# A hybrid decoder layer on one core: retention outputs turned into DRAM by VectorE, their gate moved to GpSimd in the last stage

## The chip, the cores and the metric

The kernel runs on one core of a Trainium2 chip. The time is device time of one execution in microseconds (us). Three runs of the kernel before took 2121.14, 2123.21 and 2124.8 us. The engines are PE (TensorE; PEld is its weight load), DVE (VectorE), ACT (ScalarE), POOL (GpSimd) and SP (SyncE, which here only issues DMAs). ACT and SP issue DMAs, each from its own instruction stream.

## The reference, cut to what matters

The layer has two branches on one normalised input: retention with 4 heads and latent attention (MLA). For the change only the retention branch counts. Per head, 1024 prompt tokens go through in chunks of 128, with a state of 256 x 512 that is carried on:

```
scores  = (q @ k.T) * dmask                       # 128 x 128
o       = scores @ v + (q @ s_prev) * q_decay     # 128 tokens x 512
s_new   = g**128 * s_prev + (k * k_decay).T @ v   # 256 x 512
on      = (o - mean(o)) * rsqrt(var(o) + EPS)     # per token and head
ret_out = on * gn_w * silu(rg)                    # rg: the gate path of the input projection
h_ret   = ret_out @ w_down_ret                    # 2048 -> 1024
merged  = sigmoid(ga) * h_ret + sigmoid(gb) * h_mla
```

Each head also has 32 sample tokens (8 sequences of 4) with states of their own. Data are fp32; products are made of two parts, a rounded `hi` and a rest `lo`, in three matmuls.

## The kernel before, in words

`mac` (L263) makes the three matmuls: L267 hi x hi, L268, L269. A 128-token chunk's product with 512 columns is one such triple per 128 rows of depth. The stages follow each other in the span: input norm and projections; the gate paths beside the sample's attention (to about 665 us), which leave sigmoid inputs `ga`, `gb`, the gates `mg` and the silu of the retention gate `gt` in DRAM; retention, head by head (665 to 1323); MLA of the prompt (1323 to 1625); and the last stage, in which `w_down_mla` (8 steps f), `w_down_ret` (2 halves of 8 steps) and `w_out` follow (from 1625 on).

Retention: `head_qk` (L823) projects q and k in three column tiles; each is rotated by DVE and POOL (L845 to L850), the rotated k is turned in blocks of 32 (L856) and stored to `kD` by SP (L858), and at the end of the three tiles the sample's columns are copied by ACT (`kS`, L866). `values_of` (L876) makes the values of one chunk in 8 triples, ACT casts them (`vnh`, L884), DVE takes the rest (`vnl`, L200). `front` makes scores (L939) and the decayed keys (`knh`, `knl`). `back` makes scores x values, q x old state, and keys x values into new states; then `group_norm` (L888 to L902: statistics on DVE, one power on POOL, and on ACT the row `on`, 128 tokens x 512). The steps of `back` of one chunk are woven by numbers with those of `values_of` of the next. `gate_in` (L905) loads a chunk's 128 x 4 x 128 of `gt`; `gate_out` turns `on` by four transposes on PE (L915; for the sample four products with a selecting matrix, L917), multiplies by weight and gate on DVE (L919) and stores to `go` by SP (L921). Under a head's last chunks lies the sample's state (`sample_state`, L1037); while it runs, PE is filled up with the next head's projections, in the last head with `mg`.

In the last stage, step f of `w_down_mla` loads `gate` (L1494, ACT takes its sigmoid), runs 3 column thirds of 24 matmuls, and DVE takes each third times the gate out of PSUM (L1515). Beside it a 128 x 1056 piece of `go` is loaded into `gl` (L1478), cast by ACT (`gh`, L1197) and reduced to the rest by DVE (L200).

A scheduler orders each engine's instructions beforehand, from its own estimates; on the chip every engine runs its list in order. A DMA also waits until the transfer before it on its completion lane has landed; eight lanes (DMAHW0 to DMAHW7) are shared by SP's and ACT's DMAs. PSUM has 2 buffers `mm`, 3 `ac`, 3 `tr`.

Of the kernel before, what the change touches and what calls it, by code (L numbers as in the profile page):

```python
# [162 lines left out]
def decode_step(ctx: ExitStack, tc: tile.TileContext, A: dict, O: dict):  # L163
# [17 lines left out]
    def tr():  # L181
        return banks["pool"].tile([P, 512], F32, tag="tr", name="tr", bufs=3)
# [16 lines left out]
    def lo_of(out, src, hi):  # L199
        dve.tensor_tensor(out=out, in0=src, in1=b32(hi), op=ALU.subtract)  # L200
# [16 lines left out]
    gaD = [dram.tile([P, NT], F32, tag=f"ga{f}", name=f"ga{f}") for f in range(8)]  # L217
    gbD = [dram.tile([P, NT], F32, tag=f"gb{f}", name=f"gb{f}") for f in range(8)]
    mgD = [dram.tile([P, NT], F32, tag=f"mg{f}", name=f"mg{f}") for f in range(8)]
    gtD, goD = ([dram.tile([P, 4, NT], F32, tag=f"{n}{h}", name=f"{n}{h}") for h in range(HR)] for n in ("gt", "go"))  # L220
    latD = dram.tile([NLAT // 32, 32, SEQ], F32, tag="latD", name="latD")
    xTD = dram.tile([P, 8, NT], F32, tag="xTD", name="xTD")
    pTD = dram.tile([PLE // 32, 32, NT], F32, tag="pTD", name="pTD")
# [224 lines left out]
    def chain(*gs):  # L448
        for g_ in gs:
            yield from g_  # L450
# [425 lines left out]
    def values_of(c, X, V):  # L876

        ps = mm()
        for k in range(8):
            mac(ps, tuple(x[:, c * P:(c + 1) * P] for x in xn[k]), X["W"][k], k == 0, k == 7)  # L880
            if k < 7:
                yield 0.69
        vh, vl = V[c] = pair("vn", DV, 2)
        act.copy(vh, ps)  # L884
        lo_of(vl, ps, vh)
        yield 0.69

    def group_norm(po, n, qd, qd2):  # L888
# [13 lines left out]
        act.activation(on[:n], po, AF.Identity, bias=nb[:n], scale=s[:n])  # L902
        return on

    def gate_in(h, n, cols):  # L905
        g = p4.tile([P, 4, P], F32, tag="g", name="g", bufs=3)[:, :, :n]
        sp.dma_start(g, gtD[h][:, :, cols])
        return g

    def gate_out(h, on, n, cols, g):  # L910
        pt = tr()
        for f in range(4):
            o = pt[:, f * P:f * P + n]
            if n == P:
                pe.transpose(o, on[:, f * P:(f + 1) * P], ident)  # L915
            else:
                pe.matmul(o, on[:, f * P:(f + 1) * P], C("sel"), start=True, stop=True)  # L917
        for f in range(4):
            dve.scalar_tensor_tensor(out=g[:, f, :], in0=pt[:, f * P:f * P + n], scalar=gnw[:, 4 * h + f:4 * h + f + 1],  # L919
                                     in1=g[:, f, :], op0=ALU.mult, op1=ALU.mult)  # L920
        sp.dma_start(goD[h][:, :, cols], g)  # L921

    def pair(name, w, bufs, rows_=P):
        return tuple(p4.tile([rows_, w], F32R, tag=name + s, name=name + s, bufs=bufs) for s in "hl")

    def prompt_chunks(h, X):
        q, k = X["q"], X["k"]
        V = {}
        gC = float(np.exp(P * lg[h]))
        S = p4.tile([P, 2 * DV], F32, tag="S", name="S", bufs=1)  # L930
        T = {}
        kd = C("kd", h, 1)

        def front(c):

            sl = slice(c * P, (c + 1) * P)
            pss = ac()
            for m in range(2):
                pe.matmul(pss[:, :P], k[m][:, sl], q[m][:, sl], start=m == 0, stop=m == 1)  # L939
            smh, sml = pair("sm", P, 2)  # L940
            sm = p4.tile([P, P], F32, tag="smr", name="smr", bufs=1)
            dve.tensor_tensor(out=sm, in0=pss[:, :P], in1=C("maskT", h, P), op=ALU.mult)
            act.copy(smh, sm)
            lo_of(sml, sm, smh)
            kh, kl = pair("kn", DK, 2)
            if c:
                kn = b32(kl)
                sp.dma_start(kn, kD[h % 2][4 * c:4 * c + 4].rearrange("b i f -> (b i) f"))
            else:
                kn = tr()[:, :DK]  # L950
                for m in range(2):
                    pe.transpose(kn[:, m * P:(m + 1) * P], k[m][:, sl], ident)
            act.activation(kh, kn, AF.Copy, scale=kd)
            dve.scalar_tensor_tensor(out=kl, in0=kn, scalar=kd, in1=b32(kh), op0=ALU.mult, op1=ALU.subtract)
            return smh, sml, kh, kl

        def back(c, parts):
            sl = slice(c * P, (c + 1) * P)
            smh, sml, kh, kl = parts
            vh, vl = V.pop(c)  # L960
            if c:
                qh, ql = pair("qc", DK, 1)
                for m in range(2):
                    ms = slice(m * P, (m + 1) * P)
                    hi_pool(qh[:, ms], q[m][:, sl])
                    lo_of(ql[:, ms], q[m][:, sl], qh[:, ms])
            g = gate_in(h, P, sl)
            po = ac()
            mac(po, (smh, sml), (vh, vl), True, c == 0)
            yield 0.65  # L970
            for m in range(2 if c else 0):
                Sh, Sl = T["S"]
                ms, vs = slice(m * P, (m + 1) * P), slice(m * DV, (m + 1) * DV)
                mac(po, (qh[:, ms], ql[:, ms]), (Sh[:, vs], Sl[:, vs]), False, m == 1)
                yield 0.65
            for m in range(2):
                ms, vs = slice(m * P, (m + 1) * P), slice(m * DV, (m + 1) * DV)
                pS = ac()
                mac(pS, (kh[:, ms], kl[:, ms]), (vh, vl), True, True)
                if c:  # L980
                    dve.scalar_tensor_tensor(out=S[:, vs], in0=S[:, vs], scalar=gC, in1=pS, op0=ALU.mult, op1=ALU.add)
                else:
                    act.copy(S[:, vs], pS)
                yield 0.65
            if c < 7:
                Sh, Sl = T["S"] = tuple(p4.tile([P, 2 * DV], F32R, tag="st", name=f"St{n}", bufs=4) for n in "hl")
                for m in range(2):
                    vs = slice(m * DV, (m + 1) * DV)
                    hi_pool(Sh[:, vs], S[:, vs])
                    lo_of(Sl[:, vs], S[:, vs], Sh[:, vs])  # L990
            on = group_norm(po, P, C("qd", h, 1), C("qd2", h, 1))
            yield None
            gate_out(h, on, P, sl, g)
            yield 0.43

        def ahead(u):

            for cost in u:
                if cost is None:
                    return  # L1000
                yield cost

        parts = front(0)
        yield 1.0
        yield from values_of(0, X, V)
        while late:
            gate_out(*late.pop())
        due = iter(())
        for c in range(8):
            if c == 7:  # L1010
                X["st"] = [states(h, 0, 0)]
            u = back(c, parts)
            if c < 7:
                parts = front(c + 1)
                yield 1.0
                yield from woven((chain(due, ahead(u)), 3.9), (values_of(c + 1, X, V), 5.5))
                due = u
        yield None
        yield from due
        yield from ahead(u)  # L1020
        X["st"].append(states(h, 0, 1))
        yield from u
        sp.dma_start(O["ret_prompt"][0, 0, h].rearrange("(m p) e -> p m e", p=P), S.rearrange("p (m e) -> p m e", m=2))
# [13 lines left out]
    def sample_state(h, X):  # L1037

        q, k = X["qS"], X["kS"]
        g4 = float(np.exp(NS * lg[h]))  # L1040
        sl = slice(SEQ, NT)

        def weights(k):
            raw = p4.tile([P, DV], F32, tag="vn" + "hl"[k % 2], name="wvS", bufs=2)
# [27 lines left out]
        yield 2.5  # L1072
        ps = ac()
        for n in range(8):
            for r in range(4):
# [9 lines left out]
        yield 1.0  # L1085
# [15 lines left out]
        g = gate_in(h, NR, sl)  # L1101
# [385 lines left out]

    def load_gated(f, pl):
        lo = gated(f, pl)
        return split_gated(pl("gh"), lo)  # L1490

    def gate(src, f):
        t = w4("gate", dt=F32)
# [27 lines left out]
    gx[7] = split_gated(xr_("gh"), gx[7])  # L1521
    merged, nxt = [], []
    for half in range(2):
        for f in range(8):
# [295 lines left out]
```

## Time and profile before

| | |
|---|---|
| median of three runs | 2123.21 us |
| the profiled execution: its own time, its span | 2122.66 us, 2120.9 us |
| PE busy | 2085.8 us (98%) |
| DVE, ACT, POOL busy | 1239.0, 699.6, 306.0 us |
| granted TensorE clock, mean | 0.997 |
| DMA, mean over the span | 152 GB/s |

Busy shares are averages over stages. Where PE has no gap, time goes only if PE's own work goes; where PE waits, the wait that ends last counts. "[0.44 <-X]" behind an instruction says that its engine sat idle for so long before it and that X released it.

### The profile page before, as it was taken

Reading aid. Unit: us, or ns where it says so; the run is one execution under the profiler, and the core shown is the slowest. Engines: PE = TensorE matmul, PEld = TensorE weight load, DVE = VectorE, ACT = ScalarE, POOL = GpSimd, SP = SyncE. Lnnn points to the kernel's source line nnn. Section 1 sums busy time; section 2 is a strip of 40 time slices with the busy share of each in tenths; the row PEclk is TensorE's granted clock in tenths of the full one; section 3 lists DMA queues with packets and bytes.
Section 4 is the critical chain, followed back from the end, with each engine's and each line's share of the span. In section 5 each row is a group of like instructions: output and inputs, shape, how many; then the busy total and the mean of one; then the engine's idle time right before and its main releaser. Section 6 shows DMA issues by size and latency. Waiting matters only on the chain. (4 is left out here: it accounts for less than half of the span.)

```text
span 2120.9 us, 38551 instructions
## 1 busy us (share of the span) xinstructions
PE 2085.8 (98%) x15282; PEld 1806.3 (85%) x15282; DVE 1239.0 (58%) x2791; ACT 699.6 (33%) x1455; POOL 306.0 (14%) x517
## 2 busy tenths in 40 slices
PE   8999999999999999999999999999999999999998
PEld 7988777777777898888888887888888999999976
DVE  6524555565655457677676774877777353454443
ACT  6312232333433232222222222454566341232221
POOL 2210111111100022222222220122211000000000
PEclk9999999999999999999999999999999999999999
DMA  7576656566565332654635647210112453336642
GB/s 206 135 242 212 238 193 233 208 246 227 193 240 182 113 87 71 206 163 140 208 87 163 195 147 251 56 48 19 39 52 81 152 181 94 95 117 133 175 151 91
DMA packets 346870, 321.91 MB, mean 152 GB/s; under 512 B 126945, under 2 KB 294049, under 8 KB 342593
## 3 DMA queue, kind: packets, MB, share of 16 engines
q1 hardware_dynamic: 320192, 213.92, 34.5%
q0 software_dynamic: 9216, 83.89, 10.6%
q10 hardware_dynamic: 17280, 21.63, 2.8%
q8 instruction: 120, 1.97, 0.4%
q14 instruction: 62, 0.50, 0.1%
HBM read 246.69 MB, written 72.69 MB: 151 GB/s over the span
## 5 line engine op out<-in xcount | busy, mean ns | idle before, releaser
L267 PE MATMUL mm<-xh,wh 128*128 128x352 f32 x1344 | 456.7, 340 | 3.9 <-ACT gev L440 2.3
L269 PE MATMUL mm<-xh,wl 128*128 128x352 f32 x1344 | 436.5, 325 | 2.1 <-DVE wl L200 2.1
L268 PE MATMUL mm<-xl,wh 128*128 128x352 f32 x1344 | 436.6, 325 | 0.0
L267 PEld LDWEIGHTS mm<-xh,wh 128*128 128x128 f32 x1344 | 253.2, 188 | 87.4 <-issue 77.2
L269 PEld LDWEIGHTS mm<-xh,wl 128*128 128x128 f32 x1344 | 254.2, 189 | 3.9 <-DVE wl L200 2.4
L268 PEld LDWEIGHTS mm<-xl,wh 128*128 128x128 f32 x1344 | 254.3, 189 | 3.4 <-issue 2.1
L688 DVE STREAM_TRANSPOSE kt<-craw 128x512 f32<-128x512 f32 x256 | 161.3, 681 | 85.9 <-PE sc L692 81.1
L200 DVE TENSOR_TENSOR wl<-wr,wh 128x512 fp32r<-128x512 f32 (+2 forms) x203 | 139.3, 699 | 98.1 <-ACT wh L248 67.1
L248 ACT CAST wh<-wr 128x512 fp32r<-128x512 f32 x150 | 90.0, 618 | 240.5 <-PE mm L268 184.6
L440 ACT ACTIVATE gev<-mm 128x352 f32<-128x352 f32 x120 | 55.5, 463 | 238.8 <-PE mm L269 218.4
L267 PE MATMUL mm<-mh,wh 128*128 128x352 f32 x384 | 124.5, 324 | 1.4 <-ACT mh L1197 0.8
L268 PE MATMUL mm<-ml,wh 128*128 128x352 f32 x384 | 124.8, 325 | 0.8 <-DVE ml L200 0.6
L269 PE MATMUL mm<-mh,wl 128*128 128x352 f32 x384 | 124.3, 324 | 0.0
L269 PE MATMUL mm<-gh,wl 128*128 128x352 f32 x384 | 124.3, 324 | 0.0
L267 PE MATMUL mm<-gh,wh 128*128 128x352 f32 x384 | 124.3, 324 | 0.0
L268 PE MATMUL mm<-gl,wh 128*128 128x352 f32 x384 | 124.2, 323 | 0.0
L267 PE MATMUL mm<-wv,xh 128*128 128x512 f32 x256 | 103.5, 404 | 0.0
L268 PE MATMUL mm<-wv,xh 128*128 128x512 f32 x256 | 100.9, 394 | 0.0
L269 PE MATMUL mm<-wv,xl 128*128 128x512 f32 x256 | 100.8, 394 | 0.0
L692 PE MATMUL sc<-kt,q 32*32 32x512 f32 x2560 | 91.2, 600 | 0.0
L902 ACT ACTIVATE on<-ac,gb,gs 128x512 f32<-128x512 f32 x36 | 28.0, 778 | 153.1 <-DVE gb L900 147.9
L267 PEld LDWEIGHTS mm<-mh,wh 128*128 128x128 f32 x384 | 72.4, 188 | 1.9 <-ACT mh L1197 1.0
(419 smaller groups left out, 4365.6 us busy)
## 6 DMA issues: line engine op xcount, KB each, us to landing
wr<-in_w_in_dram SPq DMA_DIRECT2D x144, 256.0 KB, 3.7
st<-in_state_ret_dram SPq DMA_DIRECT2D x32, 512.0 KB, 5.1
out_ret_sample_dram<-st SPq DMA_DIRECT2D x32, 512.0 KB, 3.5
gt<-gev ACTq DMA_DIRECT2D x48, 176.0 KB, 3.1
gl<-go SPq DMA_DIRECT2D x16, 528.0 KB, 5.4
gate<-ga SPq DMA_DIRECT2D x16, 528.0 KB, 3.6
g<-gt SPq DMA_DIRECT2D x32, 256.0 KB, 3.2
go<-g SPq DMA_DIRECT2D x32, 256.0 KB, 2.6
```

The source lines that it names most:

```text
L200: dve.tensor_tensor(out=out, in0=src, in1=b32(hi), op=ALU.subtract)
L248: hi_by[0](hi, raw)
L267: pe.matmul(out, wh, xh, start=first, stop=False)
L268: pe.matmul(out, wh, xl, start=False, stop=False)
L269: pe.matmul(out, wl, xh, start=False, stop=last)
L440: act.activation(t, ps, func)
L688: dve.transpose(kt[:, 2 * i + s].rearrange("p (n r) -> p n r", r=32), src)
L692: pe.matmul(sc[32 * v:32 * v + 32, q, :], Q["q4"][qs_, j + v // 2, 2 * (g % 2) + v % 2, :], kt[qs_, v, :], start=n == 0, stop=n == NJ // 2 ...
L902: act.activation(on[:n], po, AF.Identity, bias=nb[:n], scale=s[:n])
```

## The change

The four transposes and the selecting products on PE, the gate loads, the four DVE products and the SP store of each chunk go. Instead DVE turns `on` by one 128 x 512 transpose in blocks of 32 x 32 into a buffer `g`, and ACT issues four DMAs per chunk, one for each 32 partitions, which put the blocks into `go` in DRAM (16 blocks of 32 x 1056). These four are held, in program order, right behind ACT's cast of the next values. In the last stage `gated` loads the piece of `go` and also the piece of `gt` (into `rg`, one of three buffers that the gates use too), POOL multiplies them in three thirds, ACT makes `hi` with the norm's weight as its scale, and DVE the rest. In `back` keys x values come first, then the other two products; the numbers of the weave follow, and the first chunk's order is its own.

```diff
-    gtD, goD = ([dram.tile([P, 4, NT], F32, tag=f"{n}{h}", name=f"{n}{h}") for h in range(HR)] for n in ("gt", "go"))
+    gtD = [dram.tile([P, 4, NT], F32, tag=f"gt{h}", name=f"gt{h}") for h in range(HR)]
+    goD = [dram.tile([DV // 32, 32, NT], F32, tag=f"go{h}", name=f"go{h}") for h in range(HR)]
...
         vh, vl = V[c] = pair("vn", DV, 2)
-        act.copy(vh, ps)
+        tc.keep_in_program_order(act.copy(vh, ps))
         lo_of(vl, ps, vh)
+        store_out()
...
-    def gate_in(h, n, cols):
...
-    def gate_out(h, on, n, cols, g):
...
+    turned_out = []
+
+    def turn_out(h, on, n, t0):
+        st = p4.tile([P, DV], F32, tag="g", name="g", bufs=3).rearrange("p (b r) -> p b r", r=32)
+        dve.transpose(st, on.rearrange("p (b r) -> p b r", r=32))
+        turned_out.append((h, st, n, t0))
+
+    def store_out():
+        while turned_out:
+            h, st, n, t0 = turned_out.pop(0)
+            for a in range(4):
+                tc.keep_in_program_order(act.dma_start(goD[h][:, :, t0 + a * n:t0 + a * n + n].rearrange("b i t -> i b t"),
+                                                       st[32 * a:32 * a + 32, :, :n]))
...
+            old = T.get("S")
             for m in range(2):
                 ms, vs = slice(m * P, (m + 1) * P), slice(m * DV, (m + 1) * DV)
                 pS = ac()
...
+            po = ac()
+            mac(po, (smh, sml), (vh, vl), True, c == 0)
+            yield 0.65
+            for m in range(2 if c else 0):
+                Sh, Sl = old
+                ms, vs = slice(m * P, (m + 1) * P), slice(m * DV, (m + 1) * DV)
+                mac(po, (qh[:, ms], ql[:, ms]), (Sh[:, vs], Sl[:, vs]), False, m == 1)
+                yield 0.65
             on = group_norm(po, P, C("qd", h, 1), C("qd2", h, 1))
             yield None
-            gate_out(h, on, P, sl, g)
-            yield 0.43
+            turn_out(h, on, 32, c * P)
...
-                yield from woven((chain(due, ahead(u)), 3.9), (values_of(c + 1, X, V), 5.5))
+                if c:
+                    parts = front(c + 1)
+                    yield 1.0
+                coming = values_of(c + 1, X, V)
+                if c == 0:
+                    yield from islice(coming, 3)
+                both = woven((chain(due, ahead(u)), 3.5), (coming, 9.0))
...
         if h + 1 < HR:
-            late.append((h, on, NR, sl, g))
+            late.append((h, on, NS * 2, SEQ))
         else:
-            gate_out(h, on, NR, sl, g)
-            yield 0.5
+            store_out()
+            turn_out(h, on, NS * 2, SEQ)
+            store_out()
...
     def gated(f, pl):
         lo = pl("gl")
-        sp.dma_start(b32(lo), goD[f // 4][:, f % 4, :])
-        return lo
+        sp.dma_start(b32(lo), goD[f // 4][4 * (f % 4):4 * (f % 4) + 4].rearrange("b i t -> (b i) t"))
+        g = w4("rg", dt=F32)
+        sp.dma_start(g, gtD[f // 4][:, f % 4, :])
+        for j in range(3):
+            sl = slice(j * TH, (j + 1) * TH)
+            pool.tensor_tensor(out=g[:, sl], in0=b32(lo)[:, sl], in1=g[:, sl], op=ALU.mult)
+        return lo, g, gnw[:, f:f + 1]
 
-    def split_gated(hi, lo):
+    def split_gated(hi, lo, g, nw):
 
         for j in range(3):
             sl = slice(j * TH, (j + 1) * TH)
-            split(b32(lo)[:, sl], hi[:, sl], lo[:, sl])
+            act.activation(hi[:, sl], g[:, sl], AF.Copy, scale=nw)
+            dve.scalar_tensor_tensor(out=lo[:, sl], in0=g[:, sl], scalar=nw, in1=b32(hi)[:, sl], op0=ALU.mult, op1=ALU.subtract)
         return hi, lo
```

Behind L217 the changed kernel's lines are a few numbers off those of before. Three places show how instructions move.

ACT at the start of the second head, before: the casts of the first two chunks' values (`vnh`), the first state (`S`, twice) and the two copies `kS` of the sample's keys.

```order
L953 ACTIVATE knh<-tr,cst 128x256
L943 CAST smh<-smr 128x128
L884 CAST vnh<-mm 128x512
L953 ACTIVATE knh<-knl,cst 128x256
L943 CAST smh<-smr 128x128
L983 COPY S<-ac 128x512
L902 ACTIVATE on<-ac,gb,gs 128x512
L983 COPY S<-ac 128x512
L866 COPY kS<-k_9640 128x32
L884 CAST vnh<-mm 128x512
L943 CAST smh<-smr 128x128
L866 COPY kS<-k_9639 128x32
```

The same place of the changed kernel; the eight stores are those of the last two chunks of the head before.

```order
L885 CAST vnh<-mm 128x512
L918 DMA go_102<-g 32x16x32 x4
L867 COPY kS<-k_9558 128x32
L918 DMA go_102<-g 32x16x32 x3
L867 COPY kS<-k_9557 128x32
L918 DMA go_102<-g 32x16x32
L967 COPY S<-ac 128x512 x2
L941 CAST smh<-smr 128x128
L951 ACTIVATE knh<-knl,cst 128x256
L885 CAST vnh<-mm 128x512
L918 DMA go_102<-g 32x16x8 x4
L904 ACTIVATE on<-ac,gb,gs 128x512
```

The second cast of values stood ahead of the second `kS` copy; it now stands behind it, the last store, both state copies and the next chunk's `smh` and `knh`.

DVE at the same place of the changed kernel: the statistics of the first chunk's outputs (L892 to L902), the last factor of the rotation of k (`rt`, L849), which POOL turns into the key that the second `kS` copy reads, and the turns of that key.

```order
L940 TENSOR_TENSOR smr<-ac,cst 128x128
L892 BN_STATS st_10022<-ac 128x6
L894 BN_AGGR mv<-st_10022 128x2
L896 TENSOR_SCALAR gv<-mv,cst 128x1
L900 TENSOR_TENSOR gs<-gr,cst 128x1
L902 SCALAR_TENSOR_TENSOR gb<-mv,gs 128x1
L849 TENSOR_TENSOR rt_9863<-rx,sinR 128x352
L857 STREAM_TRANSPOSE kb<-k_9557 128x320
```

The factor stands behind the whole of the first chunk's statistics, which wait for the first chunk's scores x values.

ACT at the end of retention, before (the last head's sample row is `on`; `lh` is the cast of MLA's latents, with which MLA begins):

```order
L902 ACTIVATE on<-ac,gb,gs 128x512
L440 ACTIVATE gev<-mm 128x352
L441 DMA mg_97<-gev 128x352
L1197 CAST krA<-krT 128x512
L440 ACTIVATE gev<-mm 128x352
L1211 CAST lh_14270<-lat 128x256
```

and in the changed kernel, with the completion lanes that each DMA waits for:

```order
L918 DMA go_105<-g 32x16x8 [waits DMAHW3_49,DVE_49]
L918 DMA go_105<-g 32x16x8 [waits DMAHW4_49]
L918 DMA go_105<-g 32x16x8 [waits DMAHW5_49]
L918 DMA go_105<-g 32x16x8 [waits DMAHW6_49]
L441 ACTIVATE gev<-mm 128x352 [waits PE_49]
```

Twelve stores (eight of two chunks, four of the sample) now stand between `on` and the cast `lh`; lane 4, for which the second of the sample's waits, was last used by SP's load of the next `w_ukv` weights, which SP issues once DVE has split the weights before them.

SP in the last stage, before (`wr` are the next weights):

```order
L1494 DMA gate<-gb_86 128x1056
L247 DMA wr<-in_w_down_mla_dram 128x4x128 x2
L1478 DMA gl<-go_102 128x1056
L1494 DMA gate<-gb_87 128x1056
L247 DMA wr<-in_w_down_mla_dram 128x4x128 x2
L1478 DMA gl<-go_102 128x1056
```

and in the changed kernel:

```order
L1487 DMA rg<-gt_98 128x1056
L1507 DMA gate<-gb_86 128x1056
L248 DMA wr<-in_w_down_mla_dram 128x4x128 x2
L1485 DMA gl<-go_102 128x1056
L1487 DMA rg<-gt_99 128x1056
L1507 DMA gate<-gb_87 128x1056
```

Each step loads one piece more, ahead of the gate. On DVE the split of a step's `gl` stays where it was: ahead of that step's third product with the gate (L1515, then L1528).

## Rows read from the trace of the kernel before

**Rows 1.** Stretches: length; PE, PEld, DVE, ACT, POOL busy (instructions); clock, DMA, GB/s.

```profile
800.00:950.00 150.00, 149.46 (x847) 126.01 (x846) 105.03 (x246) 38.28 (x78) 36.94 (x66) 1.00 0.51 151
1630.00:1760.00 130.00, 130.00 (x806) 130.00 (x805) 60.65 (x117) 46.68 (x85) 2.61 (x1) 1.00 0.47 154
```

**Rows 2.** Line L915: durations ns min/median/max; waits before it, us, times.

```profile
L915 PE MATMUL tr<-cst,on x128: 271/273/328, 796.0 to 1277.3; 128*128 128x128 f32 x128
...
  ACT on L902: 1.5, 2
```

**Rows 3.** Timeline of PE's weight loads: start us, us, engine line op out<-in.

```profile
795.90 0.47 PEld L915 LDWEIGHTS tr<-cst,on 128*128 128x128 f32 x4
...
796.34 0.19 PEld L267 LDWEIGHTS mm<-wv,xh 128*128 128x128 f32 x1
...
924.68 1.09 PEld L917 LDWEIGHTS tr<-cst,on 128*128 128x128 f32 x8
```

**Rows 4.** Timeline at the end of a chunk's values, first head.

```profile
795.11 0.39 PE L268 MATMUL mm<-wv,xh 128*128 128x512 f32 x1
...
795.34 0.39 PE L269 MATMUL mm<-wv,xl 128*128 128x512 f32 x1
...
796.25 0.58 ACT L884 CAST vnh<-mm 128x512 fp32r<-128x512 f32 x1
...
796.86 0.69 DVE L200 TENSOR_TENSOR vnl<-mm,vnh 128x512 fp32r<-128x512 f32 x1 [0.35 <-ACT vnh L884]
```

**Rows 5.** Timeline of the last rotation of k, first head.

```profile
798.70 0.52 DVE L848 TENSOR_TENSOR rt<-rx,sinR 128x352 f32<-128x352 f32 x1
```

```profile
799.29 0.94 POOL L850 TENSOR_TENSOR k<-k,rt 128x352 f32<-128x352 f32 x1 [3.21 <-DVE rt L848]
```

**Rows 6.** Timeline of DVE in the last head's statistics.

```profile
1313.72 0.70 DVE L890 BATCH_NORM_STATS2 st<-ac 128x6 f32<-128x512 f32 x1 [2.63 <-PE ac L1109]
...
1316.72 0.17 DVE L892 BATCH_NORM_AGGREGATE mv<-st 128x2 f32<-128x6 f32 x1
...
1318.01 0.16 DVE L900 SCALAR_TENSOR_TENSOR gb<-mv,gs 128x1 f32<-128x1 f32 x1
```

**Rows 7.** Stores: the landing of L858's (128-byte runs), ACT's issue of `gt` (L441).

```profile
DMA to landing us min/median/max: 1.6/1.7/3.5
```

```profile
L441 ACTq DMA_DIRECT2D gt<-gev x48: 326/326/327, 372.2 to 646.5; - x48
```

**Rows 8.** Timeline at the end of retention; the last row: DMA, count, KB, us to landing.

```profile
1314.02 0.43 PE L267 MATMUL mm<-xh,wh 128*128 128x352 f32 x1
...
1323.32 0.32 PE L269 MATMUL mm<-xh,wl 128*128 128x352 f32 x1
...
1324.64 0.36 PE L267 MATMUL ac<-wqr,lh 128*128 128x256 f32 x1 [1.00 <-ACT lh L1211]
```

```profile
1324.52 0.38 SPq L247 DMA_DIRECT2D wr<-in_w_ukv_dram  x1
```

```profile
wr<-in_w_ukv_dram SPq DMA_DIRECT2D x2, 128.0 KB, 2.9
```

**Rows 9.** The last stage: timeline of SP, ACT and DVE; L1478's landing; POOL's L850.

```profile
1656.82 0.51 SPq L1478 DMA_DIRECT2D gl<-go  x1
...
1667.60 0.49 SPq L1478 DMA_DIRECT2D gl<-go  x1
```

```profile
1663.53 1.26 ACT L1197 CAST gh<-gl 128x352 fp32r<-128x352 f32 x3 [2.84 <-DMA gl<-go]
```

```profile
1665.36 0.52 DVE L1515 TENSOR_TENSOR M<-mm,gate 128x352 f32<-128x352 f32 x1
```

```profile
1632.34 3.04 DVE L200 TENSOR_TENSOR wl<-wr,wh 128x512 fp32r<-128x512 f32 x2 [0.44 <-ACT wh L248]
```

```profile
DMA to landing us min/median/max: 3.5/5.4/8.0
```

```profile
L850 POOL TENSOR_TENSOR k<-k,rt x12: 932/944/951, 775.9 to 1211.2; 128x352 f32<-128x352 f32 x12
```

More of the change, by code (lines that the diff above doesn't have):

```diff
@@ L903, in group_norm @@
         return on
-    def gate_in(h, n, cols):
-        g = p4.tile([P, 4, P], F32, tag="g", name="g", bufs=3)[:, :, :n]
-        sp.dma_start(g, gtD[h][:, :, cols])
-        return g
-    def gate_out(h, on, n, cols, g):
[L911 to L921, printed above, removed]
+    turned_out = []
[9 more added lines that the diff above has]
+                                                       st[32 * a:32 * a + 32, :, :n]))
     def pair(name, w, bufs, rows_=P):
@@ L960, in back @@
             vh, vl = V.pop(c)
[L961 to L975, printed above, removed]
+            old = T.get("S")
             for m in range(2):
@@ L984, in back @@
                 yield 0.65
+            if c:
+                qh, ql = pair("qc", DK, 1)
+                for m in range(2):
+                    ms = slice(m * P, (m + 1) * P)
+                    hi_pool(qh[:, ms], q[m][:, sl])
+                    lo_of(ql[:, ms], q[m][:, sl], qh[:, ms])
             if c < 7:
@@ L1006, in prompt_chunks @@
         while late:
-            gate_out(*late.pop())
-        due = iter(())
+            turn_out(*late.pop())
+        due, done = iter(()), 0.0
         for c in range(8):
@@ L1013, in prompt_chunks @@
             if c < 7:
-                parts = front(c + 1)
-                yield 1.0
-                yield from woven((chain(due, ahead(u)), 3.9), (values_of(c + 1, X, V), 5.5))
+                if c:
+                    parts = front(c + 1)
[4 more added lines that the diff above has]
+                both = woven((chain(due, ahead(u)), 3.5), (coming, 9.0))
+                for cost in both:
+                    yield cost
+                    if c == 0:
+                        done += cost
+                        if done > 3.5:
+                            parts, done = front(1), -99.0
+                            yield 1.0
                 due = u
@@ L1040, in sample_state @@
         g4 = float(np.exp(NS * lg[h]))
-        sl = slice(SEQ, NT)
         def weights(k):
@@ L1071, in sample_state @@
                 pool.tensor_copy(qm[:, m, :, i, NS * i:NS * i + NS], q[:, m].rearrange("p (r i t) -> p r i t", i=2, t=NS)[:, :, i])
-        yield 2.5
+        yield 3.5
         ps = ac()
@@ L1084, in sample_state @@
             act.copy(vs[rs, r * P:(r + 1) * P], ps[rs, :P])
-        yield 1.0
+        yield 2.0
         pt = tr()
@@ L1100, in sample_state @@
         pe.matmul(px, sm.rearrange("p r x -> p (r x)"), vs, start=True, stop=False, skip_group_check=True)
-        g = gate_in(h, NR, sl)
         out = O["ret_sample"][0].rearrange("(r i) h (m p) e -> i m h p r e", i=2, m=2)
@@ L1477, in gated @@
         lo = pl("gl")
-        sp.dma_start(b32(lo), goD[f // 4][:, f % 4, :])
-        return lo
-    def split_gated(hi, lo):
+        sp.dma_start(b32(lo), goD[f // 4][4 * (f % 4):4 * (f % 4) + 4].rearrange("b i t -> (b i) t"))
+        g = w4("rg", dt=F32)
+        sp.dma_start(g, gtD[f // 4][:, f % 4, :])
         for j in range(3):
             sl = slice(j * TH, (j + 1) * TH)
-            split(b32(lo)[:, sl], hi[:, sl], lo[:, sl])
+            pool.tensor_tensor(out=g[:, sl], in0=b32(lo)[:, sl], in1=g[:, sl], op=ALU.mult)
[5 more added lines that the diff above has]
+            dve.scalar_tensor_tensor(out=lo[:, sl], in0=g[:, sl], scalar=nw, in1=b32(hi)[:, sl], op0=ALU.mult, op1=ALU.subtract)
         return hi, lo
     def load_gated(f, pl):
-        lo = gated(f, pl)
-        return split_gated(pl("gh"), lo)
+        parts = gated(f, pl)
+        return split_gated(pl("gh"), *parts)
     def gate(src, f):
@@ L1520, in decode_step @@
     xr_ = slots(rph.enter_context(tc.tile_pool(name="x2", bufs=1, side="right")), "x2", 17)
-    gx[7] = split_gated(xr_("gh"), gx[7])
+    gx[7] = split_gated(xr_("gh"), *gx[7])
     merged, nxt = [], []
```

## The prediction, made before the changed kernel ran

> **What bounds the kernel now.** I read the busy time by stretches first. In a stretch of retention PE is busy for 149.46 of 150 us and in the last stage for 130.00 of 130, at full clock, while ACT, POOL and DVE have room [rows 1]. So in both stages time goes only if PE's own work goes or PE comes to wait. Next I read the lines that the change removes, with their waits and their place among PE's weight loads [rows 2, 3], and then, at each place where the new order puts something in a row that PE waits for, the durations of that chain [rows 4 to 9]. The sum is made against the profiled execution, 2122.66 us with a span of 2120.9; the 1.76 around the span I leave as it is. It lies 0.55 under the median of the three runs, so a time worked out from it stands for the median too.
>
> **The change part by part.**
>
> *PE's turning goes.* Four transposes hold up the next weight load from 795.90 to 796.34, 0.44 us [rows 3]; the 273 ns of one instruction overlap and are not the price [rows 2]. 128 of them are 32 x 0.44 = 14.1 us. The selecting products of a head take 1.09 [rows 3], three heads 3.3; the fourth head's stand at the end of retention, below. With them go the waits for `on`, 1.5 us [rows 2]. PE's next work is ready there, so it is all gain: -18.9, and I allow 2 us to either side.
>
> *DVE, POOL, SP in retention.* One turn on DVE in place of four products, loads and stores gone from SP: DVE was busy for 105 of 150 us [rows 1] and doesn't set the end. Nothing.
>
> *Keys x values first.* In the middle of a head the casts now have this long: after the last values matmul PE has the six matmuls of q x old state at 0.23 (795.11 to 795.34) and the scores, 0.33 (from 795.57 to the load at 795.90), 1.7 us, and one matmul more until `vnl` is read, 2.0 [rows 3, 4]. In the shown chunk the cast starts 0.68 and `vnl` ends 1.98 after the last values slot, with ACT held up a little [rows 4]. It just fits. I take nothing, and keep 0.3 per chunk as the bound: 28 chunks, 8 us. The four stores stand behind the cast, 0.33 each [rows 7], 1.3 of some 9.5 us in which ACT is a quarter busy: hidden.
>
> *The start of heads 2 to 4.* Here something is newly in a row. Count from the end of the first chunk's values. PE does 57 matmuls, 13.25, and two pairs of scores, 0.66, until it wants the second chunk's `vnh` at 13.9, and `vnl` one matmul later. DVE: scores x values of the first chunk end at 8.0 (33 matmuls, one pair of scores); its statistics take 0.70 and 1.45 [rows 6], to 10.15, and only then comes the last factor `rt`, 0.59 until POOL starts, 0.94 there [rows 5]: 11.7. Behind that key ACT has the copy, one store, two state copies, `smh` and `knh`, 2.3 us (0.33 for the store, 0.4 for each of the others, an estimate under the 0.58 of the larger cast [rows 4, 7]), then the cast: 14.0 to 14.6, and `vnl` by 15.3. PE waits 0.7 and then 0.5, 1.2 us a head, three heads: +3.6. If ACT is quicker or the factor earlier it is 0; with 0.58 for every one and stores of 0.5, as SP's longest here [rows 9], 2.6 a head: 8.
>
> *The end of retention.* Before, 10.62 us lie between the last state product's successor and MLA's first matmul (1314.02 to 1324.64) [rows 8], filled by 48 matmuls of `mg`. The new order leaves 39 there, so 9 x 0.161 (130 us for 806 matmuls [rows 1]) = 1.45 us of work have gone ahead. The new chain from the same point: 39 matmuls 6.3; SP issues the `w_ukv` load 1.04 behind the last of them (1323.48 to 1324.52); it lands in 2.9 [rows 8], 10.2; that frees the lane, and the sample's last three stores go, 0.67 until the last is issued, 1.7 until it lands [rows 7], 12.6; the latent's cast and PE follow, about 0.7 more as an estimate. That is 13.3 against 10.62 - 1.45 = 9.17: +4.2. Without the wait for the lane the twelve stores would be through 4 us after `on`, and it is +2; with issues of 0.5 and landings of 3.5, +7. The Trainium skill bears on the landing: its page DMA: Bandwidth & Descriptors (Specifications) asks for 512 bytes or more per transfer for full rate, and the sample's stores have runs of 32. The 128-byte runs of `kD` land in 1.7 [rows 7], so no row shows the rule at this size; by it the term would go to its upper end.
>
> *The last stage.* DVE's order puts the split of a step's `gl` ahead of the third product of that step, and the next loads wait for that product. Before, that ring takes 10.78 (1656.82 to 1667.60) [rows 9], less than the 72 x 0.161 = 11.6 of PE's step [rows 1]. Now three POOL products of 0.94 stand between landing and cast; from landing to the third product there were 1.83 (1663.53 to 1665.36), and there are 2.83 + 0.9, +1.9. The `rg` piece goes ahead of `gl` in the queue: the landing of `gl` takes 6.7 behind 1040 KB and 3.5 at best [rows 9], 0.3 per 100 KB, 1.6 for 528 KB, of which 0.5 is hidden as `rg` is issued earlier: 0 to 1.1. The ring becomes 12.7 to 13.8; with the median landing, 5.4 instead of 6.7, 11.4 to 12.5. I take 12.5, 0.9 over PE. PSUM's second buffer covers the first step's lateness, then five steps pay: +4.5, between 0 and 13. In the halves of `w_down_ret` the products of a step no longer bring in the next `gl`, and I see no ring over 11.6: nothing.
>
> Sum: -18.9 + 3.6 + 4.2 + 4.5 = -6.6, so 2116.1: I say **2116**.
>
> **The rivals.**
>
> *All hidden.* The casts at the head starts come in time, the ring runs at 11.4, the stores at the end meet no lane: -18.9 + 2.0, 2105.8. For it: most of these chains sit within 1 us of being hidden, and before, PE hardly waited at all. Against it: three chains would all have to come out at their better end.
>
> *The last stage's ring is far over PE* (slower). DVE's split now reads two SBUF operands, as `wl` does; beside a POOL product `wl` took 3.04 for two [rows 9], against 0.69 for one without it [rows 4]. If the split is held by one POOL product, the ring is 13.8 + 0.94, near 14.8, 3.2 over PE in five steps: 16; with the other two terms +5, 2127.7. It passes the measurable from a ring of 14.7. If `gl` lands at 8.0, 2 more a step: 2137. Against it: the last split comes after POOL's last product. The Trainium skill has this on its page SBUF — State Buffer (Who interferes with whom): a VectorE instruction with two SBUF inputs contends with a GpSimd instruction that reads SBUF. The `wl` row agrees; by the page the first two splits of each step would be held, the third not, and the sum would stay.
>
> *Keys x values wait in every chunk.* `vnl` comes 0.3 late in 28 chunks, +8.4, 2124.5, no change. For it: by the row it fits with nothing to spare. Against it: in that row ACT was held up by a `kS` copy, which only a head's start has.
>
> **How the numbers follow.** Chances: my forecast 0.44 (its own range 2111 to 2121), all hidden 0.24, the ring 0.12, the chunks 0.12, and 0.08 for what I haven't seen, such as a long gap of PE at the end of retention that slows what follows. What differs from no change by less than 0.2% (4.2 us) a measurement of this kernel can't tell. Faster, under 2119.0: 0.24, 0.35 of the forecast's 0.44 and 0.02, in all 0.61. Slower, over 2127.5: most of the ring, a third of the chunks, a little of the rest, 0.15. Between them 0.24. The range 2105 to 2129 leaves out 0.1 on each side.
>
> **What would show it.** Right: in retention PE falls by some 17 to 20 us; at each head's second chunk the keys x values wait for `vnh` and `vnl`, about 1 us; a gap of some 6 us on PE ahead of MLA's first matmul, with ACT's stores or their landing as the releaser; in the last stage `gl` issues over 12 us apart, and PE waiting for a PSUM buffer in steps 2 to 6. Wrong: no wait at the heads, gl issues 11.6 apart, a wait for `vnl` in every chunk, or a PE saving well off 0.44 per chunk.

## The result: 9 us slower, and the profile after

The changed kernel takes 2131.72 us (median of 6 runs, 2126.71 to 2134.49) against 2122.71 for the kernel before on the same chip: ratio 1.0041, 95% interval 1.0027 to 1.0054. The prediction was 2116 and its range ended at 2129, so it is wrong in sign and size. In the changed kernel lines behind L217 stand 1 to 13 further down: the cast `vnh` is L885, `on` L904, DVE's turn L911, the stores L918, `knh` L951, the gate's load L1487, POOL's product L1490, `gh` L1497, DVE's split L1498, M L1528.

First the two stretches of [rows 1], in the changed kernel. Its profiled run took 2132.86 us, with a span of 2131.0.

```profile
800.00:950.00 150.00, 147.88 (x813) 123.32 (x813) 101.93 (x224) 36.28 (x77) 40.20 (x68) 1.00 0.49 134
1630.00:1760.00 130.00, 120.72 (x727) 118.51 (x726) 58.56 (x93) 42.22 (x66) 37.82 (x35) 0.99 0.56 184
```

PE, which had hardly a gap (0.5 of 150 us and 0.0 of 130), now stands still for 2 us in the first stretch and for 9 in the second. The view of PE's waits says for whom (us in total, times, longest; the rows behind the dots are waits in stages that the change doesn't touch):

```profile
PE ac L268 <- ACT lh L1218: 7.6, 1, 7.6
PE mm L268 <- DVE M L1528: 7.0, 6, 1.9
...
PE ac L269 <- DVE vnl L200: 3.6, 5, 1.0
...
PE mm L268 <- DVE mev L1545: 2.3, 1, 2.3
...
PE ac L268 <- ACT vnh L885: 1.1, 3, 0.4
```

All three places are ones that the prediction had priced. To weigh them I took the starts of the same PE matmuls out of both traces, so that the span falls into stages. In this table (us, worked out from the traces, one profiled execution each) the stages are: up to retention's first scores; to the turning of the last head's sample keys; to MLA's first scores; to the first `ml` matmul; to the third step of `w_down_ret`; to `w_out`; to the end of PE's last matmul, 9.0 before the end of the span.

```
               before   reten-  its     MLA     w_down_  rest of  w_out
               reten.   tion    end             mla      w_d._ret
before         781.23   496.90  70.45   246.85  139.71   255.99   120.78
after          783.85   485.31  77.39   246.54  152.50   255.99   120.44
after - before  +2.62   -11.59  +6.94    -0.31  +12.79     0.00    -0.34
e1_ring        779.67   486.10  75.99   246.60  156.93   255.99   120.97
e4_noturn      780.72   502.38  70.60   246.58  139.70   255.99   121.27
e5_later       784.55   486.50  78.22   246.55  153.03   259.83   120.65
e6_norm        787.30   485.59  72.27   246.59  149.11   257.76   120.86
e9_pin         787.90   486.25  77.04   246.46  140.50   255.99   120.78
e11_all        790.07   484.67  73.45   247.33  140.47   255.99   120.85
e12_order      788.56   519.21  72.01   246.62  139.68   255.99   120.63
```

The first column is the same code in all of them, but for the copies that e11_all moves to POOL, and goes from 779.7 to 790.1; so the 2.6 there need not be the change's. MLA and `w_out`, which no edit touches, spread by 0.9, so less than 1 us in a row says nothing. What is the change's: retention gives 11.6, its end takes 6.9 and the last stage 12.8.

**The head starts.** ACT, DVE and PE's weight loads at the second chunk of the second head (start, duration, instruction, idle before), where [rows 4] showed a cast in time:

```profile
936.29 0.22 ACT L867 COPY kS<-k 128x32 f32<-128x32 f32 x1 [6.09 <-POOL k L851]
936.30 0.31 ACTq L918 DMA_DIRECT2D go<-g  x1
936.65 0.59 ACT L967 COPY S<-ac 128x512 f32<-128x512 f32 x1
...
938.22 0.58 ACT L885 CAST vnh<-mm 128x512 fp32r<-128x512 f32 x1
```
```profile
937.97 1.08 DVE L200 TENSOR_TENSOR Stl<-S,Sth 128x512 fp32r<-128x512 f32 x1 [0.78 <-POOL Sth L197]
...
939.58 0.68 DVE L200 TENSOR_TENSOR vnl<-mm,vnh 128x512 fp32r<-128x512 f32 x1
```
```profile
938.85 0.19 PEld L268 LDWEIGHTS ac<-vnh,knh 128*128 128x128 f32 x1 [0.54 <-ACT vnh L885]
940.31 0.19 PEld L269 LDWEIGHTS ac<-vnl,knh 128*128 128x128 f32 x1 [1.27 <-DVE vnl L200]
```

ACT stands idle for 6.09 in front of `kS`, as the prediction said, and everything after that runs in a row; on DVE the low state part, `sml` and `knl` (behind the dots) go ahead of `vnl`. PE's weight loads lose 0.54 and 1.27, 1.8 at each of heads 2 to 4. The other two of the five waits for `vnl` are in the first head, 1.1 together.

**The end of retention**, chosen lines of DVE, ACT, SP and PE (compare [rows 8]):

```profile
1309.89 0.17 DVE L894 BATCH_NORM_AGGREGATE mv<-st 128x2 f32<-128x6 f32 x1
1311.38 0.78 ACT L904 ACTIVATE on<-ac,gb,gs 128x512 f32<-128x512 f32 x1 [0.99 <-DVE gb L902]
1311.38 7.90 ACTq L918 DMA_DIRECT2D go<-g  x12
1314.65 0.38 SPq L248 DMA_DIRECT2D wr<-in_w_ukv_dram  x1
1320.86 4.98 ACT L1218 CAST lh<-lat 128x256 fp32r<-128x256 f32 x11 [1.06 <-DMA go<-g]
1321.32 0.29 PEld L268 LDWEIGHTS ac<-wqr,lh 128*128 128x128 f32 x1 [7.84 <-ACT lh L1218]
```

The statistics stand behind the state products on DVE until 1309.89. Then twelve stores take ACT 7.90, the last three of them only from 1317.90, when SP's load of 1314.65 had landed (1317.88), and the latent's cast waits for the last to land. Behind the gap, and behind one in the last stage, the clock is down. Windows of the changed kernel: length, busy time of PE, PEld, DVE, ACT and POOL, then granted clock, DMA share and GB/s:

```profile
1320.00:1325.00 5.00, 3.68 (x13) 3.19 (x14) 4.10 (x10) 4.14 (x10) 1.32 (x3) 0.50 0.50 146
1325.00:1330.00 5.00, 5.00 (x22) 4.20 (x21) 4.47 (x14) 2.46 (x5) 0.00 (x0) 0.73 0.00 0
1738.00:1744.00 6.00, 4.09 (x16) 4.09 (x17) 2.58 (x5) 1.69 (x3) 1.49 (x2) 0.73 0.71 217
```

0.50 is the lower of the two levels, 1.2 GHz. In the kernel before both stretches ran at 1.00. The Trainium skill's page TensorE: Matmul & The Clock Gate (HAM oscillation) says that a wait between bursts of matmuls is paid a second time at the low clock; the rows behind the gap of 7.84 agree.

**The last stage**, one step on POOL, DVE and SP (compare [rows 9]):

```profile
1666.19 3.04 POOL L1490 TENSOR_TENSOR rg<-gl,rg 128x352 f32<-128x352 f32 x3 [9.56 <-DMA gl<-go]
```
```profile
1667.79 0.63 DVE L1498 SCALAR_TENSOR_TENSOR gl<-rg,gnw,gh 128x352 fp32r<-128x352 f32 x1 [4.70 <-ACT gh L1497]
1668.69 0.92 DVE L1498 SCALAR_TENSOR_TENSOR gl<-rg,gnw,gh 128x352 fp32r<-128x352 f32 x1 [0.28 <-ACT gh L1497]
1669.88 0.58 DVE L1498 SCALAR_TENSOR_TENSOR gl<-rg,gnw,gh 128x352 fp32r<-128x352 f32 x1 [0.27 <-ACT gh L1497]
1670.38 0.52 DVE L1528 TENSOR_TENSOR M<-mm,gate 128x352 f32<-128x352 f32 x1
```
```profile
1659.97 0.51 SPq L1485 DMA_DIRECT2D gl<-go  x1
1670.50 0.34 SPq L1487 DMA_DIRECT2D rg<-gt  x1
1670.93 0.39 SPq L1507 DMA_DIRECT2D gate<-gb  x1
...
1672.75 0.50 SPq L1485 DMA_DIRECT2D gl<-go  x1
```

DVE stands in front of the split for 4.70 and only then takes the third product M, for which PE's PSUM buffer waits; SP's next loads wait for DVE, and the ring is 12.78 (1659.97 to 1672.75). Of that, 2.25 are SP's own queue: `rg`, `gate` and two weight loads are issued ahead of the next `gl` (1670.50 to 1672.75). PE's step is 11.6. PE's matmuls of that third product were through at about 1666.4, so DVE came to it 4 us late. The Trainium skill's page PSUM — Partial Sum Buffer (Engine vs sequencer instructions) calls VectorE's queue strict FIFO; the 4.70 in front of a product that was nearly due, and then due, is that.

### The profile page after: what moved, and what is told of

It is laid out like the page before. It is cut to its first block, busy times and chain, and to the rows that moved or that the text cites. A ratio compares the mean times of both kernels' runs of the same rounds, so it can differ in the third digit from the quotient of the medians.

```text
span 2131.0 us, 38327 instructions
## 1 busy us (share of the span) xinstructions
PE 2077.8 (98%) x15122; PEld 1795.3 (84%) x15122; DVE 1232.7 (58%) x2683; ACT 702.2 (33%) x1455; POOL 357.0 (17%) x565
## 4 chain that ended last, share of the span: by engine, by line
PE 83%; issue 4%; DMA 4%; DVE 3%; POOL 3%; ACT 2%; SPq 0%; ACTq 0%; POOLq 0%; DVEq 0%
PE mm L268 20%; PE mm L269 19%; PE mm L270 19%; PE sc L693 4%; PE x L724 3%; PE ac L269 2%; DMA gl<-go 2%; PE ac L268 2%; PE mm L1390 2%; PE ac L270 2%; PE tr L1376 1%; POOL rg L1490 1%; PE ac L1115 1%; PE ac L1333 1%; PE x L718 1%
## 5 line engine op out<-in xcount | busy, mean ns | idle before, releaser
L441 ACT ACTIVATE gev<-mm 128x352 f32<-128x352 f32 x120 | 55.7, 464 | 260.4 <-PE mm L270 241.4
L1356 POOL TENSOR_SCALAR pr<-pr,rl 128x128 f32<-128x128 f32 (+3 forms) x64 | 48.2, 754 | 168.0 <-DVE rl L1355 117.9
```

The source lines that it names most:

```text
L441: act.activation(t, ps, func)
L1356: pool.tensor_scalar(p_[:, :W], p_[:, :W], rl, 1.0, op0=ALU.mult, op1=ALU.mult)
```

## The experiments

The runs are from three chips, on which the kernel before took 2122.6, 2123.9 and 2130.4 us, so ratios to the kernel before on the same chip are compared: 1.0041 is the changed kernel, and 0.001 is 2.1 us.

**e1_ring**: the gate's piece no longer holds one of the three buffers that the loads wait for.

```diff
-        g = w4("rg", dt=F32)
-        sp.dma_start(g, gtD[f // 4][:, f % 4, :])
+        r = w4("rg", dt=F32) if hi is None else b32(hi)
+        sp.dma_start(r, gtD[f // 4][:, f % 4, :])
+        g = r if hi is None else w4("rp", dt=F32)
```

> The gate's piece is loaded into the tile that later takes gh, and only POOL's product uses the ring of three buffers that it shared with the sigmoid's gates, so no load of the last stage waits for DVE's split of the step before. Theory 1 (the ring runs through that buffer: split, rg load, gate load, gl load, landing, three products, cast, split): gl issues come to 11.6 apart, PE's waits for M and mev go, with the slow clock behind the last of them: 9 to 13 us off the changed kernel's 2131.7, so 2119 to 2123. Rival (the 6 us landing and POOL's three products alone make 12.8): issues stay over 12.5 apart and the time within 2 us of 2131.7.

Ratio 1.0060 (1.0047 to 1.0074). Theory 1 fell. The rival has the issues right, over 12.5, but they were now 13.1 to 15.4 apart and the time 4 us above the changed kernel's, which it doesn't explain. SP's queue over 1632 to 1712 tells; the first row is of the changed kernel, the second of this one:

```profile
SPq L1487 <- DVE gl L1498: 51.8, 6, 9.2
```
```profile
SPq L248 <- DVE wl L200: 53.6, 5, 11.2
```

The loads had waited for DVE's split through `rg`; now they waited behind a weight load, for `wl`, which DVE takes after the same split. So the ring closes through DVE, and freeing the buffer didn't open it.

**e5_later**: the loads written a step ahead of product and split, with two small buffers for the products.

```diff
+        ahead.append(loads_gated(f, xs_, f == 7))
+        if f:
+            gx.append(finish(*ahead.pop(0)))
```

> The last stage apart: the gate's piece lands in the tile that later takes gh, POOL's products go by thirds through two small buffers, and product, cast and split of a step's tile are written one step behind its loads; so no load of the stage waits for DVE's split, and DVE's split finds its tile landed. The first run on this stage, e1_ring, had freed only the buffer and the ring had gone on by the weight loads, at 13 to 14 a step. Theory 1 (the ring is closed by DVE, in order: split of the tile just loaded, third product, low weights, behind which SP issues the next loads): with the split's tile a step old, PE's 9.3 of waits for M and mev go, and the slow clock behind the last one: 11 to 13 us off 2131.7, so 2118.5 to 2121. Rival (PE waits there because POOL's products and the added load slow everything that DVE and the DMA engines do): more than half of the waits stay, 2126 or more.

Ratio 1.0071 (1.0057 to 1.0085): theory 1 missed as well. Written a step later, the splits were still placed ahead of the third product (why the scheduler did so isn't shown), and SP now waited for the products themselves:

```profile
SPq L1504 <- DVE M L1525: 40.4, 4, 10.9
```

So on the chip the loads didn't come earlier: `gl` issued at 1662.33 lands at 1668.43, its gate's piece at 1669.67, and POOL's first product of that tile starts at 1669.83, with DVE's split at 1671.43 waiting for it. What an earlier load would do this run doesn't show.

**e9_pin**: the place in DVE's order.

```diff
-            ... dve.tensor_tensor(out=out[:, sl], in0=ps, in1=gb[:, sl], op=ALU.mult) ...
+            ... tc.keep_in_program_order(dve.tensor_tensor(out=out[:, sl], ...)) ...
-            dve.scalar_tensor_tensor(out=lo[:, sl], in0=g[:, sl], scalar=nw, ...)
+            tc.keep_in_program_order(dve.scalar_tensor_tensor(out=lo[:, sl], ...))
```

> The changed kernel with one thing pinned in DVE's order: in the last stage the three splits of a step's tile stand behind that step's third product M, not ahead of it. Loads, buffers and POOL's products are as in the changed kernel. e1_ring and e5_later had other buffers and earlier loads, the splits still stood ahead of the third product, and the ring went on at 13 to 14. Theory 1 (that place closes the ring: split of a tile that has not landed, third product behind it, gates and weights loaded behind that, next tile behind these): gl issues come down from 12.8 apart to PE's 11.6, the 7.0 of waits for M go, with 2.3 for mev and the slow clock behind it: 9 to 13 us off 2131.7, so 2119 to 2123. Rival (landing, POOL and the weights queued behind the split make the ring wherever the split stands): PE's waits move from M to the low weights wl, and the time stays within 3 us.

Ratio 0.9985 (0.9974 to 0.9995), 0.0056 or 11.9 us under the changed kernel, as theory 1 has it. In the stage table the last stage is 140.5, 0.8 over the kernel before. Third product, then three splits, and the wait on PE over 1625 to 1790:

```profile
1668.33 0.52 DVE L1528 TENSOR_TENSOR M<-mm,gate 128x352 f32<-128x352 f32 x1 [3.36 <-PE mm L270]
1668.77 1.57 DVE L1498 SCALAR_TENSOR_TENSOR gl<-rg,gnw,gh 128x352 fp32r<-128x352 f32 x3
```
```profile
PE mm L268 <- DVE M L1528: 0.5, 1, 0.5
```

DVE's product now waits for PE, and the splits find their data; from 1670.76 on the `gl` issues are 11.65 apart. So the added load and POOL's products cost 0.8 at most by themselves, and 12 us were a matter of order. But the scheduler moved a second thing in this run: SP now issues the next `gl` ahead of the two weight loads, not behind them, about 1 us of the ring:

```profile
1670.76 0.42 SPq L1485 DMA_DIRECT2D gl<-go  x1
1671.27 0.93 SPq L248 DMA_DIRECT2D wr<-in_w_down_mla_dram  x2
```

That alone could bring 12.8 near 11.6. The pair e8_all and e10_all_later, below, tells the two apart.

**e2_early** and **e6_norm**: the end of retention. The second adds to the first that the statistics stand ahead of three state products.

```diff
+        if h + 1 == HR:
+            store_out()
         px = ac()
...
+            if n == 3 and h + 1 == HR:
+                on = group_norm(px, P, C("qdS", h, 1), C("qd2S", h, 1))
             pd = [ac(), ac(), tr(), tr()]
```

> The eight stores of the last head's chunks 6 and 7 are issued ahead of the sample's loop instead of behind its normalisation; the sample's own four stay where they are. Theory 1 (the last four stores are late because eight go ahead of them on ACT, 0.5 each): PE's wait for the first latent cast falls from 7.6 to about 3.5, with less of the slow clock behind it: 4 to 8 us off 2131.7, so 2124 to 2128. Rival (the wait for a DMA lane, held by SP's w_ukv load, sets it): the wait stays over 6 and the time within 2 us of 2131.7.

> As e2_early, and the last sample's normalisation is written ahead of its last four state products, so that its statistics stand in front of three of them in DVE's order. Theory 1 (what is left of the gap, 4.7, is the chain statistics, normalised tile, turn, stores, landing, cast): PE's wait for the first latent cast falls by about 2, from 4.7 to under 3, and the time by 2 to 4 below e2_early's 2128.5: 2124.5 to 2126.5. Rival (SP's w_ukv load, which lands late and holds a lane or a buffer): the wait stays at 4 to 5 and the time at 2128.

Ratios 1.0027 (1.0018 to 1.0037) and 1.0005 (0.9995 to 1.0014): 3.0 and 7.6 us under the changed kernel. PE's wait for the first latent cast, 7.6 before, in the one and in the other:

```profile
PE ac L268 <- ACT lh L1220: 4.7, 1, 4.7
```
```profile
PE ac L268 <- ACT lh L1223: 2.6, 1, 2.6
```

e2's gain is under what was expected of theory 1, while its wait fell as far as was hoped (4.7 for "about 3.5"); e6 is as theory 1 has it. Its stage is 72.27, 1.8 over the kernel before.

**e3_ks** and **e7_state**: the head starts.

```diff
-                act.copy(own[:, m], dst[m][:, SEQ:])
+                pool.tensor_copy(own[:, m], dst[m][:, SEQ:])
```

> The small copies qS and kS of a head are done by POOL instead of ACT. Theory 1 (ACT, in order behind kS, which waits for the rotation's last product on POOL, holds the state copies and the values' cast back): PE's 1.8 us at the second chunk of heads 2 to 4 fall under 0.5: 4 to 5.5 us off 2131.7, so 2126 to 2128. Rival (vnl is late because DVE's low state parts and low knl stand ahead of it): only the 0.6 in front of vnh goes, 2 us in all, 2129.7; and the 1.2 in front of vnl stays.

> As e3_ks, and the split of a head's first state is written behind the second chunk's values, its high part cast by ACT instead of POOL, so that vnl stands ahead of both low state parts on DVE. Theory 1 (the 1.0 that is left in front of vnl at heads 2 to 4 is DVE's low state part, 1.09, that stands ahead of it): it falls under 0.4 each, 2 us below e3_ks's 2129.2: 2127. Rival (the state's split, now late, holds the q x state matmuls and the third chunk's vnl instead): as much comes back one chunk later, 2129 to 2131.

Ratios 1.0030 (1.0019 to 1.0042) and 1.0032 (1.0021 to 1.0043). PE's waits over the heads were 3.6 for `vnl` and 1.1 for `vnh`; here they are, in e3 and in e7, with none for `vnh`:

```profile
PE ac L269 <- DVE vnl L200: 3.1, 5, 0.8
```
```profile
PE ac L269 <- DVE vnl L200: 3.2, 7, 0.5
```

So `kS` had held the cast on ACT, and that was the smaller part: 2.3 us, as the rival has it. The larger one, `vnl`, is set by DVE, but moving the state's split away only spread it over seven places: again the rival. Most of this term wasn't undone.

**e4_noturn** and **e12_order**: the two halves of the change in retention, each alone. In e4 the gate's products read the normalised tile, so the turning is left out; e12 has the new order with the old turning and gating.

```diff
-        pt = tr()
-        for f in range(4):
-            ... pe.transpose(o, on[:, f * P:(f + 1) * P], ident) ...
-            dve.scalar_tensor_tensor(..., in0=pt[:, f * P:f * P + n], ...)
+            dve.scalar_tensor_tensor(..., in0=on[:, f * P:f * P + n], ...)
```

> The kernel before with its 128 transposes and the samples' selecting products left out: the gate's products read the normalised tile itself, so the turning is the part that is left out. Theory 1 (PE's turning is worth what the prediction took, 0.44 per four and 1.09 per sample plus the waits): 18.9 us and the last head's 1.5 off 2122.7, so 2102 to 2105. Rival (part of it was hidden and about 12 is all that there is to win, as the landmarks of the two traces say at first sight): 2109 to 2112.

> The kernel before with the keys x values first and the changed kernel's weaving, while PE still turns the outputs and VectorE still gates them (nothing left out). Theory 1 (the prediction's: the new order by itself costs nothing in a chunk, and a head's start costs 1 to 2): 2122 to 2128. Rival (the new order shortens what the casts have in every chunk, so that the turning taken off PE is partly paid back as waits): 2130 or more.

Ratios 1.0033 (1.0020 to 1.0046) and 1.0124 (1.0104 to 1.0145): each half alone is slower than the kernel before, and in e4 both theories are wrong. PE's waits in e4, then in e12:

```profile
PE ac L268 <- DVE vnl L200: 9.3, 20, 1.2
PE ac L267 <- ACT vnh L884: 3.2, 5, 0.9
```
```profile
PE tr L915 <- ACT on L902: 15.6, 25, 1.8
```

In the new order `on` comes later in the chunk, and a turning on PE waits for it in 25 places. In e4 PE waits for `vnl` in 20 chunks, and DVE's order says why; the first two rows are of the kernel before, the last two the same place of e4:

```profile
964.62 0.69 DVE L200 TENSOR_TENSOR vnl<-mm,vnh 128x512 fp32r<-128x512 f32 x1
...
966.42 1.12 DVE L919 SCALAR_TENSOR_TENSOR g<-tr,gnw,g 128x128 f32<-128x128 f32 x4
```
```profile
966.50 0.96 DVE L912 SCALAR_TENSOR_TENSOR g<-on,gnw,g 128x128 f32<-128x128 f32 x2
967.39 0.68 DVE L200 TENSOR_TENSOR vnl<-mm,vnh 128x512 fp32r<-128x512 f32 x1
```

The four gating products stood behind `vnl`; freed from PE's turning, two or three of them stand directly ahead of it in 17 of the 20 chunks. The cast ends at 966.75, so without them `vnl` would be through at about 967.5 (an estimate from these rows), which is when PE wants it. So e4 doesn't show that PE's turning covered the cast, nor what the turning is worth alone: it shows another order. Retention is 5.5 us longer in e4 and 22.3 in e12, and 11.6 shorter with both edits. The waits of the view don't add up to all of it: in e4 12.5 are named where 18.9 + 5.5 would be needed. Counted from one matmul's start to the next, PE loses 0.73 at `vnl` in such a chunk of e4, where the view has 0.46. The gating products, which now read SBUF, take 398 ns in the mean where they took 330.

**e8_all**, **e10_all_later** and **e11_all**: combinations. e8 is e5, e6 and e3 together, e10 that with e9's pins, e11 is e9, e6 and e3.

> The edits of e5_later, e6_norm and e3_ks together. Theory 1 (the changed kernel is the prediction's gain of PE's turning, less three rings that can be undone one by one): 12 + 6 + 2.5 off 2131.7, about 2111, faster than the kernel before by 0.5%. Rival (the three share a cause, such as the clock, or the time comes back elsewhere): 2117 or more.

> e8_all (loads a step ahead of the split, early stores, the sample's normalisation first, small copies on POOL) with the splits pinned behind the third product. Theory 1: the ring of the last stage goes wholly, 11 to 15 off e8_all's 2133.7: 2117 to 2122, or lower. Rival (it is the loads that keep PE waiting, not the place of the split): 2130 or more.

> e9_pin, e6_norm and e3_ks together, three edits of order and engine and none of buffers. Theory 1 (the three terms that the prediction had too small add up and can each be undone): 2131.7 less 10 less 7 less 2.5, so 2110 to 2114, 0.4 to 0.6% faster than the kernel before. Rival (what is won in the last stage is lost again in the halves, or the clock): 2118 or more.

Ratios 1.0043 (1.0030 to 1.0056), 0.9987 (0.9976 to 0.9998) and 0.9967 (0.9950 to 0.9984). e8 kept e5's ring and with it all of the loss; the pins alone, in e10, took 0.0056 off it. In these two SP's loads stand in the same order throughout `w_down_mla`, `gl` behind the weights, and so do POOL's and PE's instructions; DVE's order differs by the pins (a few low weights and ACT's sigmoids moved with them). The stage up to the third step of `w_down_ret` falls from 156.9 to 141.9. PE's waits over 1625 to 1790, in e8 and then in e10:

```profile
PE mm L268 <- DVE M L1530: 11.5, 6, 3.5
```
```profile
PE mm L268 <- ACT gh L1503: 1.0, 1, 1.0
PE mm L269 <- DVE gl L1504: 0.7, 1, 0.7
```

No wait for M is left. So the place of the splits in DVE's order makes the loss and takes it away with SP's queue unchanged. e11 is 0.33% or 7 us faster than the kernel before and 0.74% than the changed one. That is less than the 0.5% expected, though inside its interval's reach: against the kernel before it has 12.2 less in retention, 3.0 more at its end, 0.8 more in the last stage (stage table).

## Why the prediction was wrong, step by step

- *PE's turning goes, -18.9*: right in its place. In the middle of a head the first values matmuls of two chunks were 9.94 apart and are 9.49, 0.45 for the 0.44 taken. Up to the last head's sample 18.4 of the term should show; 11.6 do, and 6.5 of PE's waits at the head starts stand against them, 18.1.
- *Keys x values first, nothing*: right in the changed kernel, by the same 9.49; only the third chunk of heads 2 to 4 still loses about 0.3. The step was priced for a PE that no longer turns, and holds for that alone: with the turning left on PE the same order costs 26 us (e12, ratio 1.0124).
- *The start of heads 2 to 4, +3.6*: mechanism right, 6.5 measured. "PE waits 0.7 and then 0.5" was 0.54 and then 1.27, since DVE takes the low state part, 1.08, then `sml` and `knl` ahead of `vnl`; and the first head, left out, pays 1.1. (The upper bound, 2.6 a head, comes to 2.2 by its own durations: five of 0.58 and a store of 0.5 in place of 2.3.)
- *The end of retention, +4.2* (4.1 by its own figures): 6.9. The chain was right link by link (twelve stores, the last three behind SP's load, landing, cast). From the last state product to PE's next work were 14.1 (1307.19 to 1321.32), where 13.3 had been worked out; the stretch in front, with the nine matmuls, is 2.1 longer where 1.45 were counted; and from MLA's first matmul to its first scores 1.3 more pass, at the low clock behind the gap, for which there was no term.
- *The last stage, +4.5*: this is the step that failed, 12.8. The ring itself was nearly right, 12.8 for "I take 12.5". Wrong was what follows from it: "PSUM's second buffer covers the first step's lateness, then five steps pay". The first wait is the longest, 1.9, and all six gaps are paid (7.95 between PE's matmuls); "in the halves ... nothing" left out the next gap, 2.5, in the first steps of `w_down_ret`; and the low clock behind that is 1.6 (0.27 of 6 us). These make 12.1 of the 12.8. e9 shows that the term hangs together, as 11.9 go with it, and e8 and e10 that DVE's order is what ties PE to the ring.
- *The rival of the ring far over PE* gave 2127.7 and came nearest, for another reason: its price was a ring of 14.8 with the splits held by POOL. Only the second split is longer (0.92 beside 0.63 and 0.58). The old split, too, read two SBUF operands (`gl` and `gh`); new was POOL's work beside it. (Its "2 more a step" for a landing at 8.0 is 1.3 against the 6.7 that the ring has.)

The terms as measured: -18.1 + 6.5 + 6.9 + 12.8 - 0.6 = +7.5 from retention on (the 0.6 is MLA and `w_out`, untouched), and 2.6 before it, 10.1 between the two profiled executions. The sum had -6.6; of the 14.1 between, 8.3 are the last stage's.

## What to carry to other kernels

When a new operand is handed to an engine that runs in order, ask first what stands behind it there: three splits placed ahead of a product that PE waits for made 12 us, and freeing the buffer of the load didn't help, while the place did. A ring just over the bound of a step is paid at every turn, so an estimate of 0.9 over needs its count of turns checked up to the next place that drains it; whether the low clock comes on top differed between the kernels here. Two edits that were planned together can't be priced by running each alone when the order is made anew around each: both halves were slower than the kernel before, by waits that the changed kernel doesn't have.

## What the runs showed of the hardware

- PE's clock went to its lower level within the wait of 7.8 and behind that of 2.5, and stayed at 1.00 in every 10 us of the stretch before the latter, with its six waits of 7.0 in all, 1.9 the longest. The length of the wait alone doesn't settle it: in e6_norm the granted clock was 0.83 over 1640 to 1650, behind a wait of 1.7, and in e2_early it was 1.00 from 1660 to 1680, with a wait of 2.5 in it.
- The sample's stores have runs of 32 bytes, which the prediction feared; the last, issued at 1318.79, landed at 1320.68, 1.89 later, where 1.7 had been taken. The chunks' stores, of 128 bytes, are in the same median. At the end of retention it was the sum of the issues, some 0.5 each on ACT, and the wait for the lane that counted:

```profile
L918 ACTq DMA_DIRECT2D go<-g x144: 309/501/807, 807.6 to 1318.8; - x144
DMA to landing us min/median/max: 1.7/1.9/10.3
```
